# Weight sums written over the raw weight tile, and a copy moved earlier, in a two-block transformer kernel

## The chip, the cores and the metric

The kernel runs on one core of one Trainium2 chip. What counts is the device time of one execution, in microseconds. The core's engines work side by side and each takes its own instructions in order: TensorE (PE) multiplies matrices, its weight loads shown apart as PEld; VectorE (DVE) and ScalarE (ACT) do elementwise work; GpSimd (POOL) does little here; SyncE (SP) issues the transfers. An instruction that has to wait holds up everything behind it on its engine.

## The reference, cut to what matters

Two transformer blocks follow each other on 256 tokens of width 2048, batch 1, all in float32. The parts in which the change works are the two feed-forward networks; around them stand attention, retention, a gating unit and a recurrent unit that the change touches only through the order of their work.

```python
hf = rmsnorm(x, norm_ffn_g[l])                                   # block 1
x = x + (jax.nn.silu(hf @ w_gate[l]) * (hf @ w_up[l])) @ w_down[l]
...
h = _rmsnorm(x, norm2_g[l])                                      # block 2
up = jnp.einsum('bsd,df->bsf', h, ffn_w_up[l])
up = _causal_dwconv(up, ffn_conv_w[l], ffn_conv_b[l])            # 3 taps along the tokens
gate, val = jnp.split(up, 2, axis=-1)
x = x + jnp.einsum('bsf,fd->bsd', jax.nn.gelu(gate) * val, ffn_w_down[l])
```

`w_gate` and `w_up` are 2048 x 5632, `w_down` 5632 x 2048; in block 2 the gate and value halves of `ffn_w_up` are 2048 x 6144 each.

## The kernel before, in words

**Products.** Each float32 operand is split into a rounded high part and the remainder, and `mm3` (L197) forms a product with three matmuls (L199, L200, L201): high by high, high by low, low by high. For an activation a rounded tile `r` and its remainder `r`, for a weight `wh` (high, cast by ACT at L181) and `wl` (low, subtracted by DVE at L182, which needs the cast).

**Weights.** `seq` (L244) lists the weights' units in the order of use. A unit is one transfer of 1 MB into a raw tile `w` of 128 x 2048, which is four blocks of 512 columns; `fetch` (L282) issues it on SP, and there are three such tiles. `push` (L292) makes *pieces* of a unit: `wh` and `wl` tiles of 128 x 1024, out of two pools with five tiles each, so that the cast of a piece waits until PE has done with a piece some five before it. `half` (L332) keeps four pieces made ahead of the one in use.

**Two kinds of unit.** The feed-forward weights hold two blocks of each of two matrices in a unit, and 2 x 2 block products are formed from them. An N unit is the plain way: two pieces, eight products. An S unit does with seven products of sums (Winograd's form of Strassen): pieces a, c, b, d, of which c is one block only (its tiles are called `r`), and b and d are made of sums of the four raw blocks. DVE forms the sums: L317 (128 x 1024) writes the two blocks for b into a tile `wt`, L322 and L323 (128 x 512 each) the two for d into another `wt`. 73 units are of kind S: three of eight in w_gu (`KINDS`), two of eight in w_uv (`KINDS2`), the rest in the down projections.

**Groups.** `quad_group` (L504) makes 512 columns of both matrices, for 256 tokens, in eight units: 11 groups for w_gu (block 1) and 12 for w_uv (block 2, here numbered uv0 to uv11, in three parts of four, the first two followed by two groups of the down projection). Its `gemm_q` (L423) collects seven accumulators in PSUM: M2, M4, M5, M3 in a pool of four banks (`pg`), M1, M6, M7 in another (`pp`). After the last S unit of the group `early` (L510) copies M1 on ACT (L511) and adds M6 and M7 on DVE (L512, L513). When all products are done, `finish` (L518) adds M2 to the copy of M1 (L519), then M4 (L522) and M5 (L524, L525). The next group's first product needs the bank of M2, that is, it waits for L519. `add_quads` (L565) does the like for the down projections.

**The order of the work.** No order is written by hand. A scheduler takes the instructions in the order in which the code issues them, with costs of its own, and lays down a fixed order for each engine. `tc.issue_after(behind[0])` (L316) holds L317 of an S unit behind L522 of the group before.

**Beside the products.** The result of a group goes on in the background, a step per `tick` of the next group: PE transposes it (L1220), ACT and DVE do the three-tap convolution (L1205, L1208), gelu (L1225) and product (L1226), and `Quad` (L109) splits it for the down projection and forms the sums of its blocks (L132 to L135, and their split at L181 and L182).

## Time and profile before

| what | value |
|---|---|
| median of 3 runs | 2591.85 us (2591.35 to 2593.89) |
| profiled execution, its own time | 2591.56 us |
| its span in the profile | 2589.8 us |
| granted TensorE clock, mean | 0.994 |
| PE busy | 2548.3 us, 98% |
| DVE busy | 1964.9 us, 76% |
| ACT busy | 1447.5 us, 56% |
| bytes read | 486.39 MB, 189 GB/s |
| S units / casts of weights to 128 x 1024 | 73 / 826 from raw tiles, 146 from tiles of sums |

The profile shows one execution. Each instruction has its engine, its line in the kernel, its start and duration, and, where its engine stood idle ahead of it, what released it. A matmul of 512 columns is shown with 0.39 us, but such matmuls overlap: the start of one to the start of the next is 0.23 us, and this distance is what counts. The view of waits sums up, for one line, the idle time ahead of it by what ended it; the timeline lists instructions one by one.

### The profile page before, as it was taken

To read this page: it belongs to the slowest core of one execution; us is meant where nothing else is said; L and a number is where in the kernel's file an instruction comes from. 1 tells how busy PE (TensorE), PEld (TensorE's weight loads), DVE (VectorE), ACT (ScalarE), POOL (GpSimd) and SP (SyncE) were. 2 spreads that over 40 slices of the span, in tenths; PEclk is the share of its full clock that TensorE was granted. 3 is DMA by queue.
4 is the path that set the end of the run, shared out by engine and by line. 5 is a ranking of instruction groups with operands and counts; after the bars stand their busy time and mean duration, and the time that the engine had idled before them with its cause. 6 is when DMAs were issued, how large, how long until landed. Compare 5 with 4: busy or idle time off the path is not lost.

```text
span 2589.8 us, 31366 instructions
## 1 busy us (share of the span) xinstructions
PE 2548.3 (98%) x12125; PEld 2133.3 (82%) x12125; DVE 1964.9 (76%) x2511; ACT 1447.5 (56%) x1939; POOL 27.4 (1%) x34
## 2 busy tenths in 40 slices
PE   8999999999999999999999999999989998999998
PEld 7888888888888888888888888888878887888787
DVE  6666566556569898998888677867889888987885
ACT  6555554454456554555555566655655565645564
POOL 0000010000000000000000000000000000000000
PEclk9999999999999999999999999999999999999999
DMA  6455555554454655555555564555445554455453
GB/s 250 170 179 203 203 204 185 190 184 159 146 185 173 225 182 208 193 215 186 204 195 199 207 220 163 192 182 191 180 157 192 207 185 163 186 202 204 160 212 135
DMA packets 72724, 490.51 MB, mean 189 GB/s; under 512 B 8192, under 2 KB 8320, under 8 KB 14592
## 3 DMA queue, kind: packets, MB, share of 16 engines
q1 hardware_dynamic: 72576, 488.52, 52.3%
q8 instruction: 95, 1.56, 0.2%
q14 instruction: 53, 0.43, 0.0%
HBM read 486.39 MB, written 2.10 MB: 189 GB/s over the span
## 4 chain that ended last, share of the span: by engine, by line
PE 94%; DVE 3%; DMA 1%; ACT 1%; issue 1%; SPq 0%; POOL 0%; ACTq 0%; POOLq 0%; DVEq 0%
PE pg L199 23%; PE pg L200 23%; PE pg L201 23%; PE pg L375 10%; PE pg L379 5%; PE pp L201 3%; PE pp L200 3%; PE pp L199 3%; DVE wl L182 1%; PE pp L192 1%; PE pp L1220 1%; ACT wh L181 1%; DMA w<-in_w_gu_dram 0%; DMA w<-in_w_in_f_dram 0%; DVE r L182 0%
## 5 line engine op out<-in xcount | busy, mean ns | idle before, releaser
L182 DVE TENSOR_TENSOR wl<-w,wh 128x1024 fp32r<-128x1024 f32 x826 | 1005.3, 1222 | 446.0 <-ACT wh L181 441.8
L181 ACT CAST wh<-w 128x1024 fp32r<-128x1024 f32 x826 | 864.9, 1052 | 731.7 <-PE pg L201 508.7
L199 PE MATMUL pg<-wh,r 128*128 128x512 f32 x2627 | 1006.7, 393 | 22.5 <-DVE f L519 22.1
L200 PE MATMUL pg<-wl,r 128*128 128x512 f32 x2627 | 1026.5, 391 | 0.0
L201 PE MATMUL pg<-wh,r 128*128 128x512 f32 x2627 | 1023.4, 391 | 0.0
L199 PEld LDWEIGHTS pg<-wh,r 128*128 128x128 f32 x2627 | 494.8, 188 | 127.2 <-DVE f L519 20.0
L201 PEld LDWEIGHTS pg<-wh,r 128*128 128x128 f32 x2627 | 494.7, 188 | 103.2
L200 PEld LDWEIGHTS pg<-wl,r 128*128 128x128 f32 x2627 | 495.1, 188 | 100.6
L375 PE MATMUL pg<-r,wh 128*128 128x512 f32 x1152 | 312.4, 398 | 9.0 <-ACT wh L181 7.4
L181 ACT CAST wh<-wt 128x1024 fp32r<-128x1024 f32 x146 | 153.7, 1053 | 155.9 <-PE pg L201 100.2
L375 PEld LDWEIGHTS pg<-r,wh 128*128 128x128 f32 x1152 | 202.5, 190 | 41.0 <-ACT wh L181 7.4
L182 DVE TENSOR_TENSOR wl<-wt,wh 128x1024 fp32r<-128x1024 f32 x146 | 178.2, 1220 | 52.0 <-ACT wh L181 49.8
L379 PEld LDWEIGHTS pg<-r,wl 128*128 128x128 f32 x1152 | 169.1, 191 | 18.3 <-ACT r L184 0.2
L379 PE MATMUL pg<-r,wl 128*128 128x256 f32 x1152 | 177.1, 284 | 0.0
L317 DVE TENSOR_TENSOR wt<-w 128x1024 f32<-128x1024 f32 x73 | 88.9, 1218 | 13.8 <-DMA w<-in_w_uv_dram 5.1
L1208 DVE SCALAR_TENSOR_TENSOR f<-pp,pr,f 128x255 f32<-128x255 f32 (+1 forms) x192 | 90.6, 477 | 8.0 <-ACT f L1205 6.6
L201 PE MATMUL pp<-wh,r 128*128 128x512 f32 x247 | 96.5, 391 | 0.0
L200 PE MATMUL pp<-wl,r 128*128 128x512 f32 x247 | 96.2, 389 | 0.0
L199 PE MATMUL pp<-wh,r 128*128 128x512 f32 x247 | 95.7, 393 | 0.0
L181 ACT CAST r<-f 128x512 fp32r<-128x512 f32 (+1 forms) x100 | 59.2, 592 | 24.6 <-DVE f L536 9.4
L181 ACT CAST r<-w 128x512 fp32r<-128x512 f32 x83 | 50.5, 616 | 38.3 <-DMA w<-in_w_gu_dram 22.4
L182 DVE TENSOR_TENSOR r<-f,r 128x512 fp32r<-128x512 f32 (+1 forms) x100 | 65.1, 651 | 5.3 <-ACT r L181 4.7
(202 smaller groups left out, 1691.3 us busy)
## 6 DMA issues: line engine op xcount, KB each, us to landing
w<-in_w_uv_dram SPq DMA_DIRECT2D x96, 1024.0 KB, 4.8
w<-in_w_gu_dram SPq DMA_DIRECT2D x88, 1024.0 KB, 4.8
w<-in_w_down_dram SPq DMA_DIRECT2D x84, 1024.0 KB, 4.8
w<-in_w_in_t_dram SPq DMA_DIRECT2D x40, 1024.0 KB, 4.8
w<-in_w_in_f_dram SPq DMA_DIRECT2D x39, 1024.0 KB, 4.8
w<-in_w_o_dram SPq DMA_DIRECT2D x16, 1024.0 KB, 4.7
w<-in_w_xk_dram SPq DMA_DIRECT2D x16, 1024.0 KB, 4.8
w<-in_w_xv_dram SPq DMA_DIRECT2D x16, 1024.0 KB, 4.8
```

The lines of the kernel that those rows point to most:

```text
L181: A.copy(hi, src)
L182: V.tensor_tensor(lo, src, hi.bitcast(F32), ALU.subtract)
L192: T.transpose(pt[:, k, t * P:(t + 1) * P], src[t][:, c + k * P:c + (k + 1) * P], ident)
L199: T.matmul(out, lhsT=lh[0], rhs=rh[0], start=start, stop=False)
L200: T.matmul(out, lhsT=lh[0], rhs=rh[1], start=False, stop=False)
L201: T.matmul(out, lhsT=lh[1], rhs=rh[0], start=False, stop=stop)
L317: V.tensor_tensor(sums["b"], b[:, 3:4, :].to_broadcast([P, 2, 512]), b[:, 0:3:2, :], ALU.subtract)
L375: T.matmul(ps[m], lhsT=hi[k][:, m * P:(m + 1) * P], rhs=ops[k].both(k % 2), start=begin and k == 0, stop=stop, skip_group_check=True)
L379: T.matmul(ps[m][:, S:], lhsT=lo[k][:, m * P:(m + 1) * P], rhs=ops[k].hi(k % 2), start=False, stop=False, skip_group_check=True)
L1208: V.scalar_tensor_tensor(y[:, j, d:], z[:, j, :S - d], col("ffn_conv_w_2", 96 * (2 - d) + c), y[:, j, d:], ALU.mult, ALU.add)
L1220: T.transpose(pt[:, k, t * P:(t + 1) * P], z[t][:, (2 * p + k) * P:(2 * p + k + 1) * P], ident)
```

## The change: what it does

The layout of a unit of the four feed-forward weights changes: its four blocks stand as a, b, b, a instead of a, a, b, b, so that an N unit's pieces take blocks 0 and 3, and 1 and 2. The sums of an S unit are no longer written to tiles of their own but over the raw blocks, when these have been read: at piece b, behind the split of a and c, L316 writes two blocks for b, and L318 and L319 two blocks for d; the splits of b and d then read the raw tile. The pool of `wt` tiles is gone, and there is a fourth raw tile. `issue_after` is gone. In N units the order of products in the second piece changes. `early` is called twice: at piece a of the last S unit, right behind the last product of M1, it copies M1 (now L508); at piece d it adds M6 and M7 (now L510 and L511). In `add_quads` the tiles of `early` are allocated ahead of the products. The number of instructions of each kind stays what it was. Line numbers shift: L181 and L182 are L180 and L181 in the changed kernel, L199 to L201 are L198 to L200, L519 is L517, and L522 is L519.

```diff
     cpool = ctx.enter_context(tc.tile_pool(name="cpool", bufs=1))
-    wraw = ctx.enter_context(tc.tile_pool(name="wraw", bufs=3))
-    wsum = ctx.enter_context(tc.tile_pool(name="wsum", bufs=2))
+    wraw = ctx.enter_context(tc.tile_pool(name="wraw", bufs=4))
     whi = ctx.enter_context(tc.tile_pool(name="whi", bufs=5))
     wlo = ctx.enter_context(tc.tile_pool(name="wlo", bufs=5))
     tpool = ctx.enter_context(tc.tile_pool(name="tpool", bufs=54))
...
 
 
     pieces = [(w, g, u, i) for w, g, u in seq for i in ((0, 1) if kind(w, u) == "N" else "acbd")]
-    raws, last, sums, behind = [], [None], {}, [None]
+    raws, last = [], [None]
 
     def fetch():
         w, g, u = seq[pos[0]]
...
                 hi = whi.tile([P, 1024], F32R, tag="h", name=nm("wh"))
                 lo = wlo.tile([P, 1024], F32R, tag="l", name=nm("wl"))
             b = raw.rearrange("p (b n) -> p b n", n=512)
-            if i == "a":
-
-                sums["b"] = wsum.tile([P, 2, 512], F32, tag="t", name=nm("wt"))
-                with tc.issue_after(behind[0]) if behind[0] is not None else nullcontext():
-                    V.tensor_tensor(sums["b"], b[:, 3:4, :].to_broadcast([P, 2, 512]), b[:, 0:3:2, :],
+            if w in (w_gu, w_uv, w_down, w_down2):
+
+
+                if i == "b":
+                    V.tensor_tensor(b[:, 0:2, :], b[:, 1:2, :].to_broadcast([P, 2, 512]), b[:, 0:3:2, :],
                                     ALU.subtract)
-            if i == "c":
-
-                d = sums["d"] = wsum.tile([P, 2, 512], F32, tag="t", name=nm("wt"))
-                V.tensor_tensor(d[:, 0, :], sums["b"][:, 0, :], b[:, 2, :], ALU.subtract)
-                V.tensor_tensor(d[:, 1, :], d[:, 0, :], b[:, 1, :], ALU.add)
-            if i in ("b", "d"):
-                src = sums.pop(i).rearrange("p b n -> p (b n)")
+                    V.tensor_tensor(b[:, 2, :], b[:, 0, :], b[:, 2, :], ALU.subtract)
+                    V.tensor_tensor(b[:, 3, :], b[:, 2, :], b[:, 3, :], ALU.add)
+                src = {0: b[:, 0:4:3, :], "a": b[:, 0:4:3, :], 1: b[:, 1:3, :], "b": b[:, 0:2, :],
+                       "d": b[:, 2:4, :], "c": b[:, 2, :]}[i]
+                split(hi if i == "c" else hi.rearrange("p (b n) -> p b n", n=512),
+                      lo if i == "c" else lo.rearrange("p (b n) -> p b n", n=512), src)
             else:
-                src = raw[:, {0: slice(0, 1024), 1: slice(1024, 2048), "a": slice(0, 1024),
-                              "c": slice(1024, 1536)}[i]]
-            split(hi, lo, src)
+                split(hi, lo, raw[:, 1024 * i:1024 * i + 1024])
         feed.append((w, g, u, i, hi, lo))
 
     def half(w, g, u, i, n):
...
             a = need(acts, u)
             if ks[u] == "N":
                 plan = [(0, [(2, 0, 0, 0), (2, 0, 1, 1), (4, 1, 0, 0), (4, 1, 1, 1)]),
-                        (1, [(5, 1, 1, 0), (5, 1, 0, 1), (3, "D", 1, 0), (3, "D", 0, 1)])]
+                        (1, [(5, 1, 1, 1), (5, 1, 0, 0), (3, "D", 1, 1), (3, "D", 0, 0)])]
                 for i, ops in plan:
                     hi, lo = half(wap, g, u, i, 512)
                     for m, t, k, b in ops:
...
                     hi, lo = half(wap, g, u, i, 512)
                     for m, x, b in ops:
                         prod(m, x, (hi[b], lo[b]))
+                    if "S" not in ks[u + 1:] and i in "ad":
+                        sums_done(M, i)
                     if i in "cd":
                         tick()
-                if "S" not in ks[u + 1:]:
-                    sums_done(M)
         return M
 
     def gemm_sum(wap, g, acts, k0, sums_done):
...
             a = need(acts, u)
             if ks[u] == "N":
                 plan = [(0, [(11, a.blk(0, 0), 0), (11, a.blk(1, 0), 1), (21, a.blk(0, 1), 0), (21, a.blk(1, 1), 1)]),
-                        (1, [(22, a.blk(1, 1), 0), (22, a.blk(0, 1), 1), (12, a.blk(1, 0), 0), (12, a.blk(0, 0), 1)])]
+                        (1, [(22, a.blk(1, 1), 1), (22, a.blk(0, 1), 0), (12, a.blk(1, 0), 1), (12, a.blk(0, 0), 0)])]
             else:
                 plan = [("a", [(1, a.blk(0, 0), 0), (11, a.blk(1, 0), 1)]),
                         ("c", [(12, a.sums(3), 0)]),
...
                 hi, lo = half(wap, g, k0 + u, i, 512)
                 for m, x, b in ops:
                     prod(m, x, (hi[b], lo[b]))
+                if u == end - 1 and i in ("a", "d"):
+                    sums_done(M, i)
                 if not first <= u < end:
                     tick()
-            if u == end - 1:
-                sums_done(M)
         return M
 
     def quad_group(wap, g, acts):
...
 
         m, u2, u3 = flat(ft()), flat(ft()), flat(ft())
 
-        def early(M):
-            A.copy(m, M[1])
+        def early(M, i):
+            if i == "a":
+                A.copy(m, M[1])
+                return
             V.tensor_tensor(u2, M[6], m, ALU.add)
             V.tensor_tensor(u3, M[7], u2, ALU.add)
 
...
         def finish(then):
             V.tensor_tensor(s[0], M[2], m, ALU.add)
             then(0)
-
-            behind[0] = V.tensor_tensor(s[1], M[4], u3, ALU.add).ins
+            V.tensor_tensor(s[1], M[4], u3, ALU.add)
             then(1)
             V.tensor_tensor(u2, M[5], u2, ALU.add)
             V.tensor_tensor(u3, M[5], u3, ALU.add)
...
 
     def add_quads(wap, g, acts, k0):
 
-        def early(M):
-            m, u2, u3, v = (flat(ft()) for _ in range(4))
-            A.copy(m, M[1])
+        m, u2, u3, v = (flat(ft()) for _ in range(4)) if kind(wap, k0 + 3) == "S" else [None] * 4
+
+        def early(M, i):
+            if i == "a":
+                A.copy(m, M[1])
+                return
             V.tensor_tensor(u2, M[6], m, ALU.add)
             V.tensor_tensor(u3, M[7], u2, ALU.add)
             V.tensor_tensor(u2, M[5], u2, ALU.add)
...
         def blocks(w):
             return w.reshape(-1, 2, P, w.shape[1] // 512, 512).transpose(3, 0, 2, 1, 4)
         a, b = blocks(a), blocks(b)
-        q = np.concatenate([a, b[:, :, :, ::-1]], axis=3)
+        q = np.concatenate([a[:, :, :, :1], b, a[:, :, :, 1:]], axis=3)
         return np.ascontiguousarray(q).reshape(q.shape[0], q.shape[1], P, 2048)
 
     def pairs(w):
```

Three places of the order that results. The first is DVE at the end of uv2, from the fourth piece of the next group on (`wl_3142`; `wl_3150` is the fifth, piece a of its third unit `w_3148`, which is of kind S), `f_3118` are the sums of L132 to L135. Before:

```order
L182 TENSOR_TENSOR wl_3142_15869<-w_3138_15850,wh_3141_15868 128x1024
L182 TENSOR_TENSOR r_3117_15744<-f_3097_15643,r_3116_15743 128x512
L132 TENSOR_TENSOR f_3118_15747<-f_3097_15643 128x128
L133 TENSOR_TENSOR f_3118_15747<-f_3097_15643 128x128
L182 TENSOR_TENSOR wl_3150_15901<-w_3148_15898,wh_3149_15900 128x1024
L134 TENSOR_TENSOR f_3118_15747<-f_3097_15643,f_3118_15747 128x128
L135 TENSOR_TENSOR f_3118_15747<-f_3097_15643,f_3118_15747 128x128
L182 TENSOR_TENSOR r_3120_15753<-f_3118_15747,r_3119_15752 128x512
L512 TENSOR_TENSOR f_3067_15511<-pp_3104_15667,f_3066_15510 128x512
L513 TENSOR_TENSOR f_3068_15512<-pp_3101_15659,f_3067_15511 128x512
L519 TENSOR_TENSOR f_3143_15884<-pg_3073_15521,f_3066_15510 128x512
```

and with the change (`wl_3048` is the fourth piece, `wl_3056` the fifth, of the third unit `w_3054`):

```order
L133 TENSOR_TENSOR f_3024_15650<-f_3005_15548,f_3024_15650 128x128
L181 TENSOR_TENSOR wl_3046_15756<-w_3044_15753,wh_3045_15755 128x1024
L134 TENSOR_TENSOR f_3024_15650<-f_3005_15548,f_3024_15650 128x128
L181 TENSOR_TENSOR wl_3048_15772<-w_3044_15753,wh_3047_15771 128x1024
L181 TENSOR_TENSOR r_3026_15656<-f_3024_15650,r_3025_15655 128x512
L510 TENSOR_TENSOR f_2977_15418<-pp_3012_15572,f_2976_15417 128x512
L181 TENSOR_TENSOR wl_3056_15804<-w_3054_15801,wh_3055_15803 128x1024
L511 TENSOR_TENSOR f_2978_15419<-pp_3009_15564,f_2977_15418 128x512
L517 TENSOR_TENSOR f_3049_15787<-pg_2982_15426,f_2976_15417 128x512
```

The copy of M1 on ACT stood behind the cast `r_3119` of the sums `f_3118`, which is behind the cast of the fifth piece, `wh_3149`; it now stands behind the cast of the sums, `r_3025`, too, but ahead of the cast of the fifth piece, `wh_3055`. On DVE the fifth piece `wl` (`wl_3150`, `wl_3056`) stands ahead of L519 or L517 in both. L132 to L135 (now L131 to L134) and the split behind them have moved ahead of it. At the end of uv6 the rows read alike, before and with the change. At the end of uv3 four pieces stood ahead of L519, and with the change five stand ahead of L517, in rows that read like the second fence.

The second place is DVE at the end of uv10. Before, with `wl_4015` the fourth piece of the next group and `wl_4023` its fifth:

```order
L182 TENSOR_TENSOR wl_4015_20172<-w_4011_20153,wh_4014_20171 128x1024
L182 TENSOR_TENSOR r_3993_20056<-f_3973_19955,r_3992_20055 128x512
L182 TENSOR_TENSOR wl_4023_20204<-w_4021_20201,wh_4022_20203 128x1024
L512 TENSOR_TENSOR f_3943_19823<-pp_3980_19979,f_3942_19822 128x512
L513 TENSOR_TENSOR f_3944_19824<-pp_3977_19971,f_3943_19823 128x512
L519 TENSOR_TENSOR f_4016_20187<-pg_3949_19833,f_3942_19822 128x512
L522 TENSOR_TENSOR f_4017_20188<-pg_3950_19840,f_3944_19824 128x512
```

and with the change (`wl_3866`, `wl_3868` and `wl_3871` are the next group's first three pieces):

```order
L181 TENSOR_TENSOR r_3851_19911<-f_3833_19812,r_3850_19910 128x512
L181 TENSOR_TENSOR wl_3866_19977<-w_3864_19974,wh_3865_19976 128x1024
L510 TENSOR_TENSOR f_3805_19682<-pp_3840_19836,f_3804_19681 128x512
L181 TENSOR_TENSOR wl_3868_19993<-w_3864_19974,wh_3867_19992 128x1024
L511 TENSOR_TENSOR f_3806_19683<-pp_3837_19828,f_3805_19682 128x512
L181 TENSOR_TENSOR wl_3871_20011<-w_3869_20008,wh_3870_20010 128x1024
L517 TENSOR_TENSOR f_3874_20042<-pg_3810_19690,f_3804_19681 128x512
L519 TENSOR_TENSOR f_3875_20043<-pg_3811_19697,f_3806_19683 128x512
```

L517 now has three pieces of the next group ahead of it, not five; the fourth and fifth follow it. At the end of uv1, uv5 and uv9 there were three and are two, at the end of uv7 four and are two.

The third place is DVE in the middle of uv2, its second S unit. Before (`w_3105` is the unit; `wl_3107` is piece a, `wl_3115` b, `wl_3122` d; L317, L322 and L323 stand nine, six and three rows ahead of the first):

```order
L182 TENSOR_TENSOR wl_3107_15677<-w_3105_15674,wh_3106_15676 128x1024
L1226 TENSOR_TENSOR f_3076_15540<-f_3076_15540,f_3085_15589 128x512
L182 TENSOR_TENSOR wl_3115_15726<-wt_3108_15678,wh_3114_15725 128x1024
L182 TENSOR_TENSOR r_3095_15635<-f_3076_15540,r_3094_15634 128x512
L1208 SCALAR_TENSOR_TENSOR f_3097_15643<-pp_3096_15638,pr_82,f_3097_15643 128x255
L1208 SCALAR_TENSOR_TENSOR f_3097_15643<-pp_3096_15638,pr_82,f_3097_15643 128x254
L182 TENSOR_TENSOR wl_3122_15757<-wt_3113_15708,wh_3121_15756 128x1024
```

and with the change (`w_3013` is the unit; `wl_3015` is piece a, `wl_3021` b, `r_3019` c; d follows behind one more row, an L1226):

```order
L181 TENSOR_TENSOR wl_3015_15582<-w_3013_15579,wh_3014_15581 128x1024
L1208 SCALAR_TENSOR_TENSOR f_3005_15548<-pp_3004_15543,pr_79,f_3005_15548 128x255
L316 TENSOR_TENSOR w_3013_15579<-w_3013_15579 128x1024
L1208 SCALAR_TENSOR_TENSOR f_3005_15548<-pp_3004_15543,pr_79,f_3005_15548 128x254
L181 TENSOR_TENSOR wl_3021_15626<-w_3013_15579,wh_3020_15625 128x1024
L1208 SCALAR_TENSOR_TENSOR f_3017_15602<-pp_3016_15597,pr_79,f_3017_15602 128x255
L181 TENSOR_TENSOR r_3019_15610<-w_3013_15579,r_3018_15609 128x512
L1208 SCALAR_TENSOR_TENSOR f_3017_15602<-pp_3016_15597,pr_79,f_3017_15602 128x254
L318 TENSOR_TENSOR w_3013_15579<-w_3013_15579 128x512
L319 TENSOR_TENSOR w_3013_15579<-w_3013_15579 128x512
L1208 SCALAR_TENSOR_TENSOR f_3017_15602<-pp_3016_15597,pr_79,f_3017_15602 128x255
L1208 SCALAR_TENSOR_TENSOR f_3017_15602<-pp_3016_15597,pr_79,f_3017_15602 128x254
```

The sums stand between the splits of the same unit now, and the split of c, which stood ten rows behind that of d, stands between b's and d's.

More of the change, by code (lines that the diff above doesn't have):

```diff
@@ L1 @@
 import math
-from contextlib import ExitStack, nullcontext
+from contextlib import ExitStack
 import concourse.bass as bass
```

## The prediction

> **What bounds the kernel now.** I read the page first.
>
> ```profile
> PE 2548.3 (98%) x12125; PEld 2133.3 (82%) x12125; DVE 1964.9 (76%) x2511; ACT 1447.5 (56%) x1939; POOL 27.4 (1%) x34
> ```
>
> PE is busy for 98% of the span, and the change takes no matmul away. What it can win is PE's idle time. The view of waits for PE says where that is:
>
> ```profile
> PE pg L199 <- DVE f L519: 22.1, 8, 7.0
> PE pg L375 <- ACT wh L181: 7.4, 1, 7.4
> PE pp L235 <- DVE f L233: 2.1, 1, 2.1
> ```
>
> The second is the start (first weights), the third the first norm's statistics. The first is eight stalls at the ends of w_uv groups: the next group's first matmul waits until L519 has read M2. PE's timeline shows the three long ones (uv2, uv6, uv10) and that of uv3. Each fence has the last matmul before the stall, the first after it, and, for a long one, the first that is followed at full pace again:
>
> ```profile
> 1897.51 0.39 PE L201 MATMUL pg<-wh,r 128*128 128x512 f32 x1
> 1904.90 0.79 PE L199 MATMUL pg<-wh,r 128*128 128x512 f32 x1 [7.01 <-DVE f L519]
> 1905.49 0.63 PE L200 MATMUL pg<-wl,r 128*128 128x512 f32 x1
> 1908.64 0.39 PE L199 MATMUL pg<-wh,r 128*128 128x512 f32 x1
> ...
> 1950.45 0.39 PE L201 MATMUL pg<-wh,r 128*128 128x512 f32 x1
> 1951.93 0.47 PE L199 MATMUL pg<-wh,r 128*128 128x512 f32 x1 [1.09 <-DVE f L519]
> 1952.24 0.40 PE L200 MATMUL pg<-wl,r 128*128 128x512 f32 x1
> ...
> 2169.02 0.39 PE L201 MATMUL pg<-wh,r 128*128 128x512 f32 x1
> 2176.42 0.80 PE L199 MATMUL pg<-wh,r 128*128 128x512 f32 x1 [7.01 <-DVE f L519]
> 2181.55 0.40 PE L199 MATMUL pg<-wh,r 128*128 128x512 f32 x1
> ...
> 2441.40 0.39 PE L201 MATMUL pg<-wh,r 128*128 128x512 f32 x1
> 2446.49 0.80 PE L199 MATMUL pg<-wh,r 128*128 128x512 f32 x1 [4.70 <-DVE f L519]
> 2451.20 0.39 PE L201 MATMUL pg<-wh,r 128*128 128x512 f32 x1
> ```
>
> Unhindered, starts are 0.2275 us apart. uv2's stall therefore costs 1904.90 - 1897.51 - 0.23 = 7.16 us, uv6's 7.17, uv10's 4.86, uv3's 1.25, each 0.16 more than the idle time shown. After a long stall matmuls start 0.43 apart for a while: 1904.90 to 1908.64 is 3.74 us for nine starts that should take 2.05, 1.69 lost; at uv6 5.13 for twelve, 2.40 lost; at uv10 4.71 for eleven, 2.21 lost. After uv3's stall only the first start is late. The other four (uv1, uv5, uv7, uv9) share 22.1 - 7.01 - 7.01 - 4.70 - 1.09 = 2.3 us, with 0.16 each 2.9. In all: 8.85 + 9.57 + 7.07 + 1.25 + 2.9 = **29.6 us**, the most that mending this can bring.
>
> **Why L519 is late.** DVE and ACT at the end of uv2, where PE would have gone on at T = 1897.74:
>
> ```profile
> 1898.05 1.04 ACT L181 CAST wh<-w 128x1024 fp32r<-128x1024 f32 x1
> 1901.59 0.62 ACT L181 CAST r<-f 128x512 fp32r<-128x512 f32 x1 [2.50 <-DVE f L135]
> 1902.11 0.58 ACT L511 COPY f<-pp 128x512 f32<-128x512 f32 x1
> ...
> 1899.81 1.22 DVE L182 TENSOR_TENSOR wl<-w,wh 128x1024 fp32r<-128x1024 f32 x1
> 1902.23 0.69 DVE L182 TENSOR_TENSOR r<-f,r 128x512 fp32r<-128x512 f32 x1 [0.68 <-ACT r L181]
> 1904.17 0.68 DVE L519 TENSOR_TENSOR f<-pg,f 128x512 f32<-128x512 f32 x1
> ```
>
> The cast at 1898.05 is the next group's fifth piece; its `wh` tile is the one that the group's last products have just read, so it cannot start before T. In both engines' fixed order the chain to L519 stands behind that piece: cast, sums L132 to L135, their cast, the copy of M1, L512, L513, L519. At uv3 only the fourth piece was ahead, whose tile comes free one piece earlier:
>
> ```profile
> 1948.21 1.06 ACT L181 CAST wh<-w 128x1024 fp32r<-128x1024 f32 x1 [0.22 <-PE pg L201]
> 1950.92 1.05 ACT L181 CAST wh<-w 128x1024 fp32r<-128x1024 f32 x1 [1.65 <-PE pg L201]
> ...
> 1949.37 1.21 DVE L182 TENSOR_TENSOR wl<-w,wh 128x1024 fp32r<-128x1024 f32 x1
> 1950.50 0.68 DVE L513 TENSOR_TENSOR f<-pp,f 128x512 f32<-128x512 f32 x1
> 1951.10 0.68 DVE L519 TENSOR_TENSOR f<-pg,f 128x512 f32<-128x512 f32 x1
> ```
>
> Here T = 1950.68; the fourth piece is cast at T - 2.47, the fifth at T + 0.24.
>
> **The change, part by part.** *Group ends.* By the new order, what counts is which piece stands ahead of L517. uv1, uv5, uv9: the second, uv7: the second, uv10: the third. The third piece's tile is free one piece of 12 x 0.2275 = 2.7 us before the fourth's, so L517 is through well before T (by the rows of uv3, T + 1.25 - 2.7 = T - 1.5): these five stalls go, 2.9 + 7.07 = **10.0 us gained**. (Were the cover gone, and the fourth piece ahead again, each would cost uv3's 1.25.) uv2, uv6 and now also uv3: the fifth. Nothing but the split of this piece, L511 and L517 is left behind it, since the sums, the copy and L510 come before (the copy is not right behind M1's last product, as the code has it, but far enough ahead). Cast at T + 0.24 (row 1950.92), the start of `wl` 1.16 later (1948.21 to 1949.37), L511 1.13 after that (to 1950.50), L517 0.60 later, PE 0.83 after L517's start (1951.10 to 1951.93): T + 3.96. That is a stall of 4.0 us, not 7.2. Whether slow matmuls follow it no row says, being between 1.09 and 4.70 us idle; I take 2.1 (the mean of 1.69, 2.40 and 2.21; ends 0 and 2.4), since 3.8 us idle is nearer to 4.70: 6.1 for each. uv2 gains 8.85 - 6.1 = **2.8**, uv6 9.57 - 6.1 = **3.5**, uv3 loses 6.1 - 1.25 = **4.8**. Together the ends bring 10.0 + 2.8 + 3.5 - 4.8 = 11.5.
>
> *The sums in S units.* Their number and shapes stay. The groups of instructions:
>
> ```profile
> L317 DVE TENSOR_TENSOR wt<-w 128x1024 f32<-128x1024 f32 x73 | 88.9, 1218 | 13.8 <-DMA w<-in_w_uv_dram 5.1
> L182 DVE TENSOR_TENSOR wl<-w,wh 128x1024 fp32r<-128x1024 f32 x826 | 1005.3, 1222 | 446.0 <-ACT wh L181 441.8
> ...
> L323 DVE TENSOR_TENSOR wt<-wt,w 128x512 f32<-128x512 f32 x73 | 49.9, 684 | 0.4
> L322 DVE TENSOR_TENSOR wt<-wt,w 128x512 f32<-128x512 f32 x73 | 49.9, 683 | 0.1
> ```
>
> L317 reads its blocks with a gap between and takes 1218 ns, a plain split 1222, so reads with a stride cost nothing here. Writing in place is not seen on a raw tile; L323 does it on `wt` and takes 684, L322, which does not, 683: 0 again. What changes is their place in a chain. In uv2's second S unit, before (an L1208, DVE's splits of a, b and d, and the matmul that first reads d's `wl`):
>
> ```profile
> 1873.88 0.48 DVE L1208 SCALAR_TENSOR_TENSOR f<-pp,pr,f 128x254 f32<-128x254 f32 x1
> 1874.27 1.22 DVE L182 TENSOR_TENSOR wl<-w,wh 128x1024 fp32r<-128x1024 f32 x1
> ...
> 1877.22 1.23 DVE L182 TENSOR_TENSOR wl<-wt,wh 128x1024 fp32r<-128x1024 f32 x1 [1.13 <-ACT wh L181]
> ...
> 1879.99 1.23 DVE L182 TENSOR_TENSOR wl<-wt,wh 128x1024 fp32r<-128x1024 f32 x1
> ...
> 1885.00 0.39 PE L200 MATMUL pp<-wl,r 128*128 128x512 f32 x1
> ```
>
> From a's split to the end of d's: 1881.22 - 1874.27 = 6.95 us, 3.8 to spare. With the change the rows of the order give, at DVE's distances of 1.13 (1024 columns), 0.60 (512) and 0.40 (L1208, 1873.88 to 1874.27): a 1.13, L1208 0.40, L316 1.13, L1208 0.40, a hole of 0.75 since b's cast (1.05 and 0.1) begins only at L316's end, b 1.13, L1208 0.40, c 0.60, L1208 0.40, L318 and L319 1.30, two L1208 0.80, L1226 0.60, d 1.23: 10.27. It ends at 1884.54, 0.46 before use. So no stall by the rows, but no room: between 0 and, if each of the five L1208 is 0.2 late, 0.5. For twelve such units in w_uv I take 0.2 each, **2.4 lost** (ends 0 and 6). The w_gu and down units have less between, one or two splits instead of the L1208, and I take 0.
>
> *Fourth raw tile.* It is held until d is split, later than before, and there is one more, so SP runs about one unit further ahead. DVE's waits for weights (5.1 us at L317) may shrink; they lie beside PE's work, since PE's only wait for weights is the 7.4 us at the start, so 0. At the start a weight unit now goes ahead of two loads of x, and the last L631 of the squares stands behind two more splits:
>
> ```profile
> 31.87 2.35 DVE L182 TENSOR_TENSOR wl<-w,wh 128x1024 fp32r<-128x1024 f32 x2
> 35.22 0.16 DVE L641 TENSOR_SCALAR s<-pp 128x2 f32<-128x2 f32 x1 [1.00 <-PE pp L638]
> 37.25 0.73 PE L235 MATMUL pp<-f,ones 128*128 128x256 f32 x2 [2.07 <-DVE f L233]
> ```
>
> PE waits there already, so it shows: between 0 and 2.35, middle **1.2 lost**. *The other edits* (the order of products in N units, tiles of `add_quads` ahead of time): 0; PE shows no wait at the ends of `add_quads` to win or lose.
>
> Sum against the profiled execution: 2591.56 - 11.5 + 2.4 + 1.2 = **2583.7 us**; that execution is 0.3 under the median.
>
> [...] The slow pace above is 0.43 us a start against 0.23. [...]
>
> **Rivals.** (a) *No slow matmuls after the three gaps of 3.8 us*: 3 x 2.1 = 6.3 less, 2577.4. For it, that PE lost nothing after 1.09; against it, that the loss does not grow with the gap (2.21 after 4.70, 1.69 after 7.01), so that it seems to be there or not, and 3.8 is nearer to 4.70. (b) *The change does away with all stalls*, as if the fifth piece were cast before T: 2591.6 - 29.6 = 2562. Against it: the `wh` pools still have five tiles, and the order has the piece ahead of L517. (c) *Even*: new waits in S units of 0.5 us at the twelve, and as much again at the first S units, give back 24 x 0.5 = 12 less the 2.4 counted, or half of it: 2588 to 2593. For it, 0.46 us of room. (d) *Slower*: the in-place chain decides. From b's and d's being 0.46 later than worked out, PE waits in every S unit of w_uv. L316 can't begin before a's split and holds b's cast on ACT, where L1205 queues behind it, and L1208 waits for L1205 on DVE, ahead of d. At 0.75 for each of 24 units: 18 us, 2583.7 - 2.4 + 18 = 2599. For it: ACT waits already for DVE and DVE for ACT (441.8 us on the page). Against: most of that is waiting for PE passed on.
>
> **How the numbers follow.** Forecast 0.42, (a) 0.16, (b) 0.04, (c) 0.22, (d) 0.16. A measurement of this kernel tells 0.2%, 5.2 us, from no change. Forecast, (a) and (b) are faster, but a fifth of the forecast's own spread (S units up to 6, start 2.35) passes 2586.7: faster 0.54. Same: that fifth and (c), 0.30. Slower: (d), 0.16. The range runs from 2574 (under (a), with S units and start at 0) to 2597 (most of (c), half of (d)); the forecast's own is 2578 to 2588.
>
> **What will show it.** In the waits for PE, L198 behind L517: three waits of 3.5 to 4.2 us at uv2, uv3 and uv6 and none at the other five, right; more of them, or longer than 4.5, wrong. Matmuls 0.43 apart after them, or not: rival (a). New waits of PE for `wl` or `wh` in groups of w_uv: (c) or (d). PE's wait for the statistics near 35 us: 2.1 to 4.5. A long stall left at uv10, or L517's waits of 7 us again, would make the forecast wrong.

## The result, and the profile after

| | before | changed |
|---|---|---|
| median of 3 runs, us | 2591.85 | 2628.24 (2626.39 to 2628.59) |
| ratio, with its 95% interval | | 1.0136 (1.0113 to 1.0159) |
| span of the profiled execution, us | 2589.8 | 2626.2 |

The change makes the kernel 36 us slower. The prediction said 2583.7, with 2597 as the upper end. The page's busy times of the changed kernel:

```profile
PE 2569.0 (98%) x12125; PEld 2136.7 (81%) x12125; DVE 1975.0 (75%) x2511; ACT 1440.0 (55%) x1939; POOL 26.9 (1%) x34
```

and its view of waits for PE (us in total, times, longest):

```profile
PE pp L198 <- ACT wh L180: 16.9, 16, 1.9
PE pg L198 <- DVE f L517: 11.3, 3, 3.8
PE pg L371 <- ACT wh L180: 7.5, 1, 7.5
PE pg L198 <- ACT wh L180: 3.4, 16, 0.2
PE pp L198 <- DVE f L1208: 2.8, 2, 1.7
```

L517 (the old L519) is waited for three times now, 11.3 us, where it was eight times and 22.1. But sixteen waits for a cast of weights by ACT have come (first line), which were not there before: the accumulator is in `pp`, and the matmul is the first of an S unit's piece d (M6).

Where the 36 us come from, by the distance from each matmul's start to the next beyond the usual one, which takes in the slow matmuls after a stall (worked out from both timelines):

| place | before | changed | difference |
|---|---|---|---|
| ends of w_uv groups, waits for M2's bank | 30.1 | 16.3 | -13.8 |
| S units in w_uv groups, nine stalls of 2.5 to 4.7 | 0 | 33.6 | +33.6 |
| down projections behind w_uv, four stalls | 0 | 7.4 | +7.4 |
| block 1's feed-forward part, five stalls of 1.0 to 1.5 | 0.7 | 6.6 | +5.9 |
| start, up to the statistics | 8.4 | 10.9 | +2.5 |

One of the nine, in uv2's second S unit, which the prediction had walked through. DVE and ACT, and of PE the transposition, the last matmul before the stall and the first after it:

```profile
1884.38 1.23 DVE L181 TENSOR_TENSOR wl<-w,wh 128x1024 fp32r<-128x1024 f32 x1 [0.71 <-ACT wh L180]
1885.92 1.21 DVE L316 TENSOR_TENSOR w<-w 128x1024 f32<-128x1024 f32 x1
1888.31 1.23 DVE L181 TENSOR_TENSOR wl<-w,wh 128x1024 fp32r<-128x1024 f32 x1 [0.78 <-ACT wh L180]
1893.36 0.48 DVE L1208 SCALAR_TENSOR_TENSOR f<-pp,pr,f 128x255 f32<-128x255 f32 x1 [3.83 <-ACT f L1205]
1893.86 0.69 DVE L181 TENSOR_TENSOR r<-w,r 128x512 fp32r<-128x512 f32 x1
1894.86 0.68 DVE L318 TENSOR_TENSOR w<-w 128x512 f32<-128x512 f32 x1
1895.58 0.69 DVE L319 TENSOR_TENSOR w<-w 128x512 f32<-128x512 f32 x1
...
1892.76 0.56 ACT L1205 ACTIVATE f<-pp,pr 128x256 f32<-128x256 f32 x1 [3.96 <-PE pp L1220]
1893.22 0.61 ACT L180 CAST r<-w 128x512 fp32r<-128x512 f32 x1
1896.31 4.84 ACT L180 CAST wh<-w 128x1024 fp32r<-128x1024 f32 x5 [0.76 <-DVE w L319]
...
1892.12 0.60 PE L1220 MATMUL pp<-ident,f 128*128 128x128 f32 x4
1895.56 0.39 PE L200 MATMUL pg<-r,r 128*128 128x512 f32 x1
1897.40 0.50 PE L198 MATMUL pp<-wh,r 128*128 128x512 f32 x1 [1.46 <-ACT wh L180]
```

DVE is through with b's split at 1889.5 and then does nothing for 3.8 us: the next instruction in its order is an L1208 of the convolution, which waits for L1205 on ACT, which waits for PE's transposition (L1220). PE does that at 1892.12, since the order has put it behind the first matmul of piece a of the same S unit. From there the chain runs L1205, L1208, split of c, L1208, L318, L319, cast of d: 1892.76 to 1897.35, 4.6 us. PE has 14 matmuls to do from the transposition to piece d, 3.2 us. PE waits for work that waits for PE. All nine stalls have such an L1208 ahead of the split of c, with 3.6 to 4.3 us of waiting for L1205. The waits of ACT and DVE sum it up, in the changed kernel

```profile
DVE f L1208 <- ACT f L1205: 37.4, 13, 4.3
ACT wh L180 <- DVE w L316: 131.3, 52, 4.8
ACT wh L180 <- DVE w L319: 54.7, 48, 3.7
ACT f L1205 <- PE pp L1220: 44.2, 19, 4.4
```

and in the one before:

```profile
DVE f L1208 <- ACT f L1205: 6.6, 4, 2.0
ACT wh L181 <- DVE wt L323: 27.6, 15, 4.0
ACT f L1205 <- PE pp L1220: 9.5, 6, 2.6
```

Why the split of c counts: L318 writes over c's raw block, so it must come behind the split of c, and that stands behind the background work. With a tile for the sums, L322 and L323 only read that block, and stood six and three rows ahead of a's split.

The instructions themselves cost what they did, within 6 ns (1218, 684 and 683 before):

```profile
L316 DVE TENSOR_TENSOR w<-w 128x1024 f32<-128x1024 f32 x73 | 89.1, 1220 | 1.1
L319 DVE TENSOR_TENSOR w<-w 128x512 f32<-128x512 f32 x73 | 50.4, 690 | 1.9
L318 DVE TENSOR_TENSOR w<-w 128x512 f32<-128x512 f32 x73 | 50.1, 687 | 1.1
```

### The profile page after: what moved, and what is told of

It reads as the page before. It is cut to its first block, busy times and chain, and to the rows that moved or that the text cites. A ratio compares the mean times of both kernels' runs of the same rounds, so it can differ in the third digit from the quotient of the medians.

```text
span 2626.2 us, 31426 instructions
## 1 busy us (share of the span) xinstructions
PE 2569.0 (98%) x12125; PEld 2136.7 (81%) x12125; DVE 1975.0 (75%) x2511; ACT 1440.0 (55%) x1939; POOL 26.9 (1%) x34
## 4 chain that ended last, share of the span: by engine, by line
PE 92%; DVE 5%; ACT 2%; issue 1%; DMA 0%; POOL 0%; SPq 0%; ACTq 0%; POOLq 0%; DVEq 0%
PE pg L198 22%; PE pg L199 22%; PE pg L200 22%; PE pg L371 10%; PE pg L375 5%; PE pp L199 3%; PE pp L200 2%; PE pp L198 2%; DVE wl L181 1%; ACT wh L180 1%; PE pp L191 1%; DVE r L181 1%; DVE f L1208 1%; PE pp L1220 1%; DVE w L319 0%
## 5 line engine op out<-in xcount | busy, mean ns | idle before, releaser
L181 DVE TENSOR_TENSOR wl<-w,wh 128x1024 fp32r<-128x1024 f32 x972 | 1175.1, 1222 | 493.3 <-ACT wh L180 486.9
L180 ACT CAST wh<-w 128x1024 fp32r<-128x1024 f32 x972 | 1006.3, 1051 | 884.5 <-PE pg L200 517.5
L199 PE MATMUL pg<-wl,r 128*128 128x512 f32 x2627 | 1027.4, 391 | 0.0
L200 PE MATMUL pg<-wh,r 128*128 128x512 f32 x2627 | 1024.7, 391 | 0.0
L198 PE MATMUL pg<-wh,r 128*128 128x512 f32 x2627 | 1008.4, 395 | 15.0 <-DVE f L517 11.3
L198 PEld LDWEIGHTS pg<-wh,r 128*128 128x128 f32 x2627 | 497.3, 189 | 124.8 <-issue 12.7
L200 PEld LDWEIGHTS pg<-wh,r 128*128 128x128 f32 x2627 | 495.3, 189 | 104.0
L199 PEld LDWEIGHTS pg<-wl,r 128*128 128x128 f32 x2627 | 496.1, 189 | 101.6
L1208 DVE SCALAR_TENSOR_TENSOR f<-pp,pr,f 128x255 f32<-128x255 f32 (+1 forms) x192 | 89.1, 477 | 38.8 <-ACT f L1205 37.4
L198 PE MATMUL pp<-wh,r 128*128 128x512 f32 x247 | 95.6, 402 | 19.7 <-ACT wh L180 16.9
L199 PE MATMUL pp<-wl,r 128*128 128x512 f32 x247 | 99.8, 404 | 1.7 <-DVE wl L181 1.7
L200 PE MATMUL pp<-wh,r 128*128 128x512 f32 x247 | 97.8, 396 | 0.0
L1205 ACT ACTIVATE f<-pp,pr 128x256 f32<-128x256 f32 x96 | 53.6, 561 | 75.3 <-PE pp L1220 44.2
L316 DVE TENSOR_TENSOR w<-w 128x1024 f32<-128x1024 f32 x73 | 89.1, 1220 | 1.1
L198 PEld LDWEIGHTS pp<-wh,r 128*128 128x128 f32 x247 | 46.4, 188 | 35.9 <-ACT wh L180 23.6
L180 ACT CAST r<-f 128x512 fp32r<-128x512 f32 (+1 forms) x100 | 59.2, 592 | 27.3 <-DVE f L1226 10.3
L181 DVE TENSOR_TENSOR r<-f,r 128x512 fp32r<-128x512 f32 (+1 forms) x100 | 65.2, 652 | 5.4 <-ACT r L180 4.6
L199 PEld LDWEIGHTS pp<-wl,r 128*128 128x128 f32 x247 | 46.9, 190 | 14.5 <-DVE wl L181 5.3
```

The costliest lines, as they stand in the source:

```text
L180: A.copy(hi, src)
L181: V.tensor_tensor(lo, src, hi.bitcast(F32), ALU.subtract)
L198: T.matmul(out, lhsT=lh[0], rhs=rh[0], start=start, stop=False)
L199: T.matmul(out, lhsT=lh[0], rhs=rh[1], start=False, stop=False)
L200: T.matmul(out, lhsT=lh[1], rhs=rh[0], start=False, stop=stop)
L316: V.tensor_tensor(b[:, 0:2, :], b[:, 1:2, :].to_broadcast([P, 2, 512]), b[:, 0:3:2, :], ALU.subtract)
```

## The experiments

Theory A: writing d's sums over c's block ties them to the split of c, and so to background work that in its turn waits for PE. Its rivals: the sums' new place in the code or the missing `issue_after` (B); the fourth raw tile (C); the chain from a's split over b's and d's sums being too long by itself (D). All ratios are against the kernel before, run on the same chip.

### The sums in tiles again

```diff
-    wraw = ctx.enter_context(tc.tile_pool(name="wraw", bufs=4))
+    wraw = ctx.enter_context(tc.tile_pool(name="wraw", bufs=3))
+    wsum = ctx.enter_context(tc.tile_pool(name="wsum", bufs=2))
...
                 if i == "b":
-                    V.tensor_tensor(b[:, 0:2, :], b[:, 1:2, :].to_broadcast([P, 2, 512]), b[:, 0:3:2, :],
+                    sums["b"] = wsum.tile([P, 2, 512], F32, tag="t", name=nm("wt"))
+                    V.tensor_tensor(sums["b"], b[:, 1:2, :].to_broadcast([P, 2, 512]), b[:, 0:3:2, :],
...
+                    d = sums["d"] = wsum.tile([P, 2, 512], F32, tag="t", name=nm("wt"))
+                    V.tensor_tensor(d[:, 0, :], sums["b"][:, 0, :], b[:, 2, :], ALU.subtract)
+                    V.tensor_tensor(d[:, 1, :], d[:, 0, :], b[:, 3, :], ALU.add)
```

> The changed kernel with the sums in tiles of their own again (two of 128 x 1024, three raw tiles); the new layout, the place of the sums at piece b, the earlier copy of M1 and the missing issue_after stay. Theory A (writing over the raw blocks ties d's sums to the split of c, and through it to convolution work that waits for PE): the waits of PE for d's cast in S units of w_uv, 41 us in the changed kernel, and the 6 us in w_gu are gone; at the ends of uv2 and uv6 the fifth piece and the copy behind it are back, 7 us and slow matmuls each, uv3 and uv7 1.3, uv10 4 to 7: about 2589. Theory B (the place of the sums at piece b, or issue_after being gone, makes d late): the waits in S units stay, 2620 to 2630.

Measured: 2592.6 us, ratio 1.0002 (0.9993 to 1.0012). No wait for d's cast is left anywhere. The waits at the ends are back, 23.2 us for the sum with M2 in the view of waits. Theory B falls: layout, place in the code and `issue_after` are as in the change. (Three raw tiles instead of four are the next run.) The expected time was 3.6 us off: the long waits are 7.9, 7.7 and 5.4 us, at uv2, uv6 and uv10.

### Three raw tiles, sums in place

```diff
-    wraw = ctx.enter_context(tc.tile_pool(name="wraw", bufs=4))
+    wraw = ctx.enter_context(tc.tile_pool(name="wraw", bufs=3))
```

> The changed kernel with three raw tiles in place of four. Theory A: sums over raw blocks still stand behind c's split, and on PE 17 to 19 matmuls still lie between a transposition of the convolution and the piece d whose split waits for it, so the waits in S units stay at some 45 us; the ends lose most of their waits (four pieces ahead at uv2, uv3 and uv6, two elsewhere: 1.3 each), start as before: 2592 - 30 + 4 + 45 = about 2611. Theory C (the fourth raw tile lets transfers and splits run ahead and so moves the order): waits in S units mostly gone, 2565 to 2572.

Measured: 2612.65 us, ratio 1.0077 (1.0062 to 1.0092). The stalls in S units stay, 38.0 us in block 2 (w_uv groups and down projections) and 6.8 in block 1, so theory C does not explain them. The fourth tile has a price of its own, 15.6 us between the medians and 18.0 between the profiled executions: without it the ends lose 4.7 us instead of 16.3, the start is no longer than before (3.1 less than with four), and the S units lose 2.8 less. In neither kernel does the view of PE's waits name a transfer. ACT even waits longer for transfers with three tiles (18 us for w_uv, 3 with four), beside PE's work. At the ends it is the order: four pieces instead of five stand ahead of the sum with M2.

### Only d's sums in a tile

This differs from the run before only in where d's sums go.

```diff
+    wsum = ctx.enter_context(tc.tile_pool(name="wsum", bufs=2))
...
-                    V.tensor_tensor(b[:, 2, :], b[:, 0, :], b[:, 2, :], ALU.subtract)
-                    V.tensor_tensor(b[:, 3, :], b[:, 2, :], b[:, 3, :], ALU.add)
+                    d = sums["d"] = wsum.tile([P, 2, 512], F32, tag="t", name=nm("wt"))
+                    V.tensor_tensor(d[:, 0, :], b[:, 0, :], b[:, 2, :], ALU.subtract)
+                    V.tensor_tensor(d[:, 1, :], d[:, 0, :], b[:, 3, :], ALU.add)
```

> The changed kernel with three raw tiles, and with the two sums for piece d in a tile of their own; the sums for b still overwrite the raw blocks. It differs from the run with three raw tiles (2613) only in where d's sums are written. Theory A (it is the overwriting of c's block that ties d's sums to c's split, and so to background work): in the order the sums for d stand right behind those for b, and c's split comes later by itself; the waits for d's cast, 43 us in w_uv and 7 in w_gu and down projections, are gone. At the ends four pieces stand ahead at uv2 and uv6 (1.3 each), five at uv3 and uv7 (4 and slow matmuls), three elsewhere: 2592 - 30 + 3 + 12 + 2 = about 2579. Theory D (overwriting a's and b's blocks is enough to make the chain too long): waits in S units stay above 20 us, 2595 or more.

Measured: 2579.52 us, ratio 0.995 (0.9936 to 0.9965), 33 us below the run it differs from by that alone. Its DVE in uv2's second S unit (L317 is the sum for b, L320 and L321 those for d, and the splits that follow are b's, d's, and at 1881.73 c's):

```profile
1871.40 1.23 DVE L182 TENSOR_TENSOR wl<-w,wh 128x1024 fp32r<-128x1024 f32 x1 [0.73 <-ACT wh L181]
1872.94 1.22 DVE L317 TENSOR_TENSOR w<-w 128x1024 f32<-128x1024 f32 x1
1874.46 0.68 DVE L320 TENSOR_TENSOR wt<-w 128x512 f32<-128x512 f32 x1
1875.18 0.69 DVE L321 TENSOR_TENSOR wt<-wt,w 128x512 f32<-128x512 f32 x1
1875.79 1.22 DVE L182 TENSOR_TENSOR wl<-w,wh 128x1024 fp32r<-128x1024 f32 x1
1877.04 1.23 DVE L182 TENSOR_TENSOR wl<-wt,wh 128x1024 fp32r<-128x1024 f32 x1
...
1881.73 0.68 DVE L182 TENSOR_TENSOR r<-w,r 128x512 fp32r<-128x512 f32 x1
```

From a's split to the end of d's it is 6.9 us, as before the change, and c's split comes 4.7 us after d's. So it is c's block being overwritten, not the writing in place as such: theory D falls too. Against the first experiment's kernel, from which this one differs only in that b's sums go over the raw blocks, it is even 13 us faster: its ends lose 16.6 us, there it was 30.9. The long waits that remain are those at the ends of uv3 and uv7, 4.4 us and 2.2 to 2.9 of slow matmuls, with five pieces ahead.

### The convolution one tick later, and every tick

In the changed kernel, first

```diff
-            spawn(conv_pairs(gate, val, g, acts, 2 * (g - g0), 1 if g == g1 - 1 else 2, g1 < PARTS2[-1][1]))
+            spawn(conv_pairs(gate, val, g, acts, 2 * (g - g0), 1 if g == g1 - 1 else 2, g1 < PARTS2[-1][1]), 1)
```

> The changed kernel with the convolution of each w_uv group spawned one tick later, nothing else. On PE no transposition of the convolution is then nearer than 31 matmuls ahead of a piece whose split waits for it, where the changed kernel has eleven at 16 to 19. Theory A: the 41 us of waits in S units of w_uv are gone, the 6 us in w_gu and the 2.5 at the start stay; at the ends of uv2, uv3, uv6 and uv7 the fifth piece and the copy behind it stand ahead of the sum with M2, 7 us and 2 of slow matmuls each: 2592 - 30 + 9 + 37 + 2 = about 2610. Theory D (the chain of sums is too long by itself, with or without the convolution): waits in S units stay, and with the longer ends 2640 to 2650.

Measured: 2624.0 us, ratio 1.0122 (1.0107 to 1.0137). Inside the w_uv groups no stall for d's cast is left; the sums for d no longer wait for a transposition. The expected time is 14 us off: the down projections keep 12.6 us of stalls, and the ends cost 42 us, among them 6.6 at uv11, which the sum had left out.

Then, instead of that, every tick:

```diff
-            spawn(conv_pairs(gate, val, g, acts, 2 * (g - g0), 1 if g == g1 - 1 else 2, g1 < PARTS2[-1][1]))
+            spawn(conv_pairs(gate, val, g, acts, 2 * (g - g0), 1, g1 < PARTS2[-1][1]))
```

> The changed kernel with the steps of the convolution one tick apart in every w_uv group, not two; nothing else. In the order no transposition is nearer than 34 matmuls to a piece that waits for it, and two or three pieces stand ahead of the sum with M2 at every end. Theory A: no waits in S units of w_uv and none at the ends; what stays is 6 us in w_gu and 2.5 more at the start: 2592 - 30 + 9 = about 2571. Theory D: the waits in S units stay, 2628 - 16 = about 2612.

Measured: 2598.07 us, ratio 1.0021 (1.0011 to 1.0031). The waits at the ends are gone, but four stalls of 4.5 to 5.8 us stand in S units; with five of 1.0 us and 6.3 in the down projections they are what puts the time above the expected 2571. DVE and PE at one of the four:

```profile
1889.85 0.29 DVE L134 TENSOR_TENSOR f<-f,f 128x128 f32<-128x128 f32 x1
1890.83 0.69 DVE L181 TENSOR_TENSOR r<-f,r 128x512 fp32r<-128x512 f32 x1 [0.69 <-ACT r L180]
1891.43 0.68 DVE L181 TENSOR_TENSOR r<-w,r 128x512 fp32r<-128x512 f32 x1
1892.15 0.69 DVE L318 TENSOR_TENSOR w<-w 128x512 f32<-128x512 f32 x1
1892.88 0.69 DVE L319 TENSOR_TENSOR w<-w 128x512 f32<-128x512 f32 x1
...
1894.70 0.50 PE L198 MATMUL pp<-wh,r 128*128 128x512 f32 x1 [1.79 <-ACT wh L180]
```

It is the same tie with other background work: the split of c (1891.43) stands behind the block sums for the down projection (L131 to L134 and their split), and L318 behind it. So theory A holds in a wider form than I gave it: not the convolution's wait for PE alone, but whatever the scheduler puts ahead of c's split.

### The split of c first

```diff
-    pieces = [(w, g, u, i) for w, g, u in seq for i in ((0, 1) if kind(w, u) == "N" else "acbd")]
+    pieces = [(w, g, u, i) for w, g, u in seq for i in ((0, 1) if kind(w, u) == "N" else "cabd")]
...
-                plan = [("a", [(1, a.blk(0, 0), 0), (2, a.blk(1, 0), 1)]),
-                        ("c", [(3, a.sums(3), 0)]),
+                plan = [("c", [(3, a.sums(3), 0)]),
+                        ("a", [(1, a.blk(0, 0), 0), (2, a.blk(1, 0), 1)]),
```

and the same in `gemm_sum`.

> The changed kernel with the pieces of an S unit in the order c, a, b, d instead of a, c, b, d, in the splits and in the products; the sums stay in the raw blocks. Theory A (d's sums are late because they overwrite c's block and so stand behind c's split, which the scheduler has put behind background work): in the order L318 and L319 now stand right behind L316, so the waits for d's cast are gone in w_uv and in w_gu, 47 us; at the ends of uv2, uv3, uv6 and uv7 four pieces stand ahead, 1.3 to 1.7 us each, elsewhere 0.5 or nothing; 2 us more at the start: 2592 - 30 + 8 + 2 = about 2572. Theory D (writing over the raw tile makes the chain to d too long in any order, since b's and d's sums wait for a's split): waits of 1 us or more in each S unit of w_uv stay, above 2595.

Measured: 2589.7 us, ratio 0.9993 (0.9984 to 1.0002). In the w_uv groups no stall for d's cast is left, as expected. In block 1 the 6.6 us stay, and in the down projections 11.6, where block sums still stand ahead of c's split; the ends cost 9.3, as about expected. The expected 2572 was too low by the first two.

With the convolution every tick as well (pause 1 in place of `1 if g == g1 - 1 else 2`):

> The kernel with pieces in the order c, a, b, d, and the convolution's steps one tick apart in every w_uv group. At every end two or three pieces stand ahead of the sum with M2 and none ahead of the copy of M1. Theory A: neither waits in S units nor at the ends; what stays is the start, 2 us more than before: about 2564. Theory D: as for the one before, less its ends: above 2587.

Measured: 2594.69 us, ratio 1.0013 (1.0003 to 1.0022), far from the expected 2564. The ends are clean, but four stalls of 3.8 to 4.2 us in S units stand there as without c first: the split of c, though first in the code, is behind L131 to L134 in the order again; block 1 and the down projections keep 6.6 and 8.3 us. The place in the code does not fix the place in the order.

### The kernel before with the convolution every tick

```diff
-            spawn(conv_pairs(gate, val, g, acts, 2 * (g - g0), 1 if g == g1 - 1 else 2, g1 < PARTS2[-1][1]))
+            spawn(conv_pairs(gate, val, g, acts, 2 * (g - g0), 1, g1 < PARTS2[-1][1]))
```

> The kernel before the change, with the convolution's steps one tick apart in every w_uv group. At the ends two or three pieces stand ahead of the sum with M2, one at uv10, none or two ahead of the copy of M1. If the waits at the ends come from the place of background work and the fifth piece, as the trace of before was read, they go, all or all but 2 us: 2562 to 2565. Rival (the waits there come from VectorE being full in w_uv groups): they move to other places, 2580 to 2592.

Measured: **2562.65 us**, ratio 0.9889 (0.9874 to 0.9903), faster than both kernels. Its longest waits of PE:

```profile
PE pg L375 <- ACT wh L181: 7.8, 1, 7.8
PE pp L235 <- DVE f L233: 2.1, 1, 2.1
```

and the stretch around uv2 (its length, then busy time of PE, PEld, DVE, ACT and POOL, granted clock, DMA share, GB/s):

```profile
1853.40:1904.90 51.50, 51.50 (x238) 42.57 (x237) 48.11 (x67) 34.20 (x44) 0.00 (x0) 1.00 0.55 197
```

No wait for M2's bank is left. DVE is busy for 48.1 of 51.5 us and PE never waits: DVE was not too full, its work stood in the wrong order.

The same line in the change with its sums in tiles, that is, in the first experiment's kernel:

> The changed kernel with the sums in tiles of their own (two, with three raw tiles) and the convolution's steps one tick apart in every w_uv group: layout, place of the sums in the code, copy of M1 and missing issue_after stay as in the change. At the ends two or three pieces stand ahead. Theory A: no waits in S units, none at the ends: 2560 to 2565, as the kernel before with the same convolution steps (2563). Theory D or B: waits in S units, 2580 or more.

Measured: 2563.73 us, ratio 0.989 (0.9875 to 0.9904), the same within the intervals.

### The copy of M1, alone and taken out

The copy's move as in the change, put into the kernel before (and the like in `add_quads`):

```diff
-        def early(M):
-            A.copy(m, M[1])
+        def early(M, i):
+            if i == "a":
+                A.copy(m, M[1])
+                return
...
+                    if "S" not in ks[u + 1:] and i in "ad":
+                        sums_done(M, i)
```

> The kernel before the change, with only the copy of M1 moved behind M1's last product (in the groups and in the down projections); sums in tiles of their own, three raw tiles, issue_after kept. The order has the same pieces ahead of the copy and of the sum with M2 at every end as before (five at uv2, uv6 and uv10), since the scheduler puts the copy behind the same casts: no change, 2590 to 2594. Rival (the copy's place in the code is what shortened the waits at the ends in the changed kernel): 14 us less, about 2578.

Measured: 2592.16 us, ratio 1.0001 (0.9991 to 1.001). And the change with the copy in its old place:

```diff
             if i == "a":
-                A.copy(m, M[1])
                 return
+            A.copy(m, M[1])
```

> The changed kernel with the copy of M1 in its old place in the code, behind piece d's products. The order has the same numbers of pieces ahead of the copy and of the sum with M2 at every end as the changed kernel: 2626 to 2630, the three waits of 3.9 us at the ends unchanged. Rival (the earlier copy is what spares the changed kernel waits at the ends): 2635 or more.

Measured: 2627.85 us, ratio 1.0137 (1.012 to 1.0154), against 2628.24 with it. The edit is worth nothing either way.

### The fifth piece held back, in the kernel before

```diff
-            split(hi, lo, src)
+            held = ExitStack()
+            for x in hold:
+                held.enter_context(tc.issue_after(x))
+            hold.clear()
+            with held:
+                split(hi, lo, src)
...
-            V.tensor_tensor(s[0], M[2], m, ALU.add)
+            hold[:] = [V.tensor_tensor(s[0], M[2], m, ALU.add).ins, copied[0]]
```

(`hold` has the sum with M2 and the copy of M1, `copied[0]`, of the group that ends.)

> The kernel before the change, with the split of the next group's fifth piece queued by issue_after behind the sum with M2 on VectorE and behind the copy of M1 on ScalarE; nothing else. In the order four pieces stand ahead at uv2, uv6 and uv10 instead of five. If the fifth piece's cast, which can't start before the group's last product, is what makes the long waits: uv2, uv6 and uv10 shrink from 25 us together to 1.3 to 2.5 each without slow matmuls: 2592 - 25 + 6 = about 2573. Rival (the chain of sums of the background split, L132 to L135, makes them): 5 us each stay, 2585 to 2592.

Measured: 2592.04 us, ratio 1.0005 (0.9996 to 1.0014): the expectation missed, its rival came. At the end of uv2 the fifth piece is out of the way, and PE still loses 6.0 us instead of 7.2. ACT and DVE there:

```profile
1895.81 1.22 DVE L182 TENSOR_TENSOR wl<-w,wh 128x1024 fp32r<-128x1024 f32 x1 [0.54 <-ACT wh L181]
1898.27 0.29 DVE L135 TENSOR_TENSOR f<-f,f 128x128 f32<-128x128 f32 x1
1901.18 0.68 DVE L524 TENSOR_TENSOR f<-pg,f 128x512 f32<-128x512 f32 x1
...
1898.60 0.62 ACT L181 CAST r<-f 128x512 fp32r<-128x512 f32 x1 [2.31 <-DVE f L135]
1899.12 0.58 ACT L516 COPY f<-pp 128x512 f32<-128x512 f32 x1
```

The copy of M1 still stands behind the cast of the block sums L132 to L135, and these behind the fourth piece's split and the end of the convolution. That chain of background work made the long waits of the kernel before; the fifth piece added 1.1 us at uv2, uv6 and uv10. What holding it back saved there, uv3 and uv7 gave back (2.7 us instead of 1.25 each, and slow matmuls at uv3).

## Why the prediction was wrong

**The ends of groups: right.** Three waits of 3.5 to 4.2 us at uv2, uv3 and uv6 and none at the other five were predicted, with 3.96 for each. PE's timeline at the first of them:

```profile
1911.82 0.39 PE L200 MATMUL pg<-wh,r 128*128 128x512 f32 x1
1915.97 0.76 PE L198 MATMUL pg<-wh,r 128*128 128x512 f32 x1 [3.77 <-DVE f L517]
```

That is 4.15 - 0.23 = 3.92 us lost, three times, with 1.4 to 1.6 of slow matmuls (2.1 taken). The gain was 13.8 us, 11.5 were predicted. Rival (a) fell: slow matmuls came, all three times (the last section has the clock granted there).

**"Why L519 is late": half right.** It named the fifth piece and the chain behind it. Holding the fifth piece alone brought nothing in sum; moving the background work, with which the pieces ahead became two or three, brought all of it. The steps about the changed kernel's ends held because there that chain had been moved ahead of the fifth piece.

**The sums in S units: this term failed**, at the step that allowed each of the five L1208 at most 0.2 us of lateness, took 0.2 us for each of twelve units and so 2.4 us in all. It took DVE's durations and added them up as though every instruction between a's split and d's had its operands. One L1208 of them had 3.8 us to wait for PE, and the order shown ahead of the prediction has it there, between b's split and c's. What the step had not asked is when that L1208's transposition stands on PE: behind the first matmul of piece a, 14 matmuls ahead of piece d. With the question asked, the sum is: 4.6 us of chain less 3.2 of matmuls, about 1.4 idle, and the trace has 1.46. The term measured 33.6 us in w_uv groups in place of 2.4, of which the slow matmuls behind the stalls are a part.

**The down projections and block 1, taken at 0:** 7.4 and 5.9. In block 1 the block sums of `Quad` and their splits play the convolution's part; the prediction called them "one or two splits instead of the L1208". Of the four stalls in the down projections, two (2.6 and 2.0 us) are ended by an L1208 itself: the matmul writes a tile in `pp`, the pool out of which L1208 reads. The other two end with d's cast, behind a product of the convolution (L1226) and its splits.

**Rival (d), the slower one,** had the right place and the wait of L1208 for L1205. It let L1205 queue behind b's cast on ACT, where the trace has it wait 3.96 us for PE. It gave 18 us for 24 units, a chance of 0.16 and 2599; nine stalls cost 33.6. Its reason against, that most of the waiting between ACT and DVE "is waiting for PE passed on", is what the nine stalls are made of. The range was too narrow because its upper end took only half of (d), and the 0.2 us a step rested on no row of the new order.

**The fourth raw tile, taken at 0 apart from the start:** it has cost 15.6 us by the run with three, most of it at the ends, over the order that the scheduler made with it. The start lost 2.5 (1.2 predicted, ends 0 and 2.35).

**The copy of M1:** worth nothing in either kernel. The prediction gave it no term of its own, and had read in the order that it does not stand where the code has it.

## What to carry to other kernels

Overwriting an input saves a tile, and adds an order: the writer must come behind every reader, and behind all that stands ahead of that reader on its engine. Where a scheduler interleaves background work, ask of each instruction on the new chain not only how long it takes but on which other engine its operand is made, and where in that engine's order: a chain that leads back to the waiting engine can be priced by counting the instructions between the two places. And when an engine that is busy for 93% of a stretch makes another wait, look at its order before its load.
